# One SBUF buffer shared in turns by the residual sum and the Strassen sums, with the HBM weight sums paced by the SP queue

## The chip, the cores and the metric

The kernel runs on one core of a Trainium2 chip. The metric is device time in microseconds (us): the median of several executions. Besides these there is one profiled execution, from which all traces below come. The engines are named as in the profile: PE (TensorE, matmuls; PEld its weight loads), DVE (VectorE), ACT (ScalarE), POOL (GpSimd), and SP (SyncE, which only issues DMAs here). "SPq", "POOLq" and "ACTq" are the sequencers that issue DMAs. Each engine carries out its own instructions in order.

## The reference

Two layers over x of 512 positions by 1024 features, in float32, each ending in `LayerNorm(ALPHA * h + sublayer(h))` with ALPHA = sqrt(2).

```python
# layer 0: one input projection (6 x 1024 columns) for two branches
q, k, v, g_ret, xb, g_lru = split(h @ w_in)
ret = group_norm(chunked_retention(rope(q), rope(k), v)) * silu(g_ret)   # 8 heads of 128
lru = rg_lru(conv4(xb)) * silu(g_lru)                                    # 8 blocks of 128
h = layer_norm(ALPHA * h + concat(ret, lru) @ w_out)
# layer 1: differential attention, 8 heads, two softmax maps each, value width 256
q, k, v, g = split(h @ w_in)                                             # 4 x 2048 columns
w = softmax(q1 k1) - lam * softmax(q2 k2)                                # causal
o = rms_norm(w @ v) * silu(g)
h = layer_norm(ALPHA * h + o @ w_out)
```

## The kernel before

**Products.** A float32 operand is split into a rounded high part and a low rest (`split`, L142: one ACT cast and one DVE subtraction, L148 and L149), and every product is three matmuls (`mm3`, L151 to L154). Weights lie in HBM as pieces of 128 x 1024 values, 512 KB each, named w0, w1, ... in the order of use. `fetch` (L166) loads a piece on SP into one of two raw buffers (`wraw`) and splits it into one of five pairs (`wsp`). `take(n)` (L181) asks for the next piece and sees to it that n more are on their way. A `t_unit` is one piece: eight k-tiles of three 128x512 matmuls; an `s_unit` is four pieces; an `out_unit` (L222) is one output projection of four pieces (two in layer 0's last parts).

**Order.** PE's and SP's instructions run in the order in which the program text issues them (manual schedule). ACT, DVE and POOL are ordered by the framework's scheduler, which may move an instruction ahead of anything that it doesn't depend on. A planner, `Side` (L48), mixes side jobs into the units: after each k-tile the unit calls `side.tick()`, and at most one waiting job then issues its next piece; a job that yields n is due again n ticks later. `side.need(job)` runs ticks until a job is done. Layer 0 has 512 ticks of its own: 40 t_units of 8, two s_units of 32, and output projections of 32, 32, 16, 16 and 32.

**Layer 0** runs the list `ev` (L254): values, then per head gates, conv inputs, q and k, with retention and RG-LRU as side jobs, and its output projections adding into `y`, a 128 x 4 x 1024 SBUF tile (2 MB, tag "y"). `even_end` (L595) normalizes y, transposes it into `h` (the input of layer 1), multiplies it by ALPHA on ACT (L605) and stores it to `yd` in HBM by eight POOL DMAs (L606).

**Layer 1** runs the list `od` (L270): v and g of heads 0 and 1, q and k of heads 0 to 2, then for g = 1, 2, 3 a "gv" unit, the output projection of a pair of heads, and q and k of the next heads. Attention runs as side jobs. A gv unit (`gates_values`, L733) makes gates and values of two heads by a Strassen-like scheme of seven block products in place of eight. It needs two kinds of sums:

- sums of weight blocks, t1 to t4 (L283 to L286), 24 pieces in all, made in HBM: a copy and then a DMA that accumulates, both issued by POOL from the side job `weight_sums` (L384), which starts at tick 30 and issues one DMA every 10 ticks;
- sums of blocks of h, four of 1 MB (`act_sums`, L695): fourteen DVE and four ACT instructions on 128 x 1024 values, issued all at once after unit g; two half buffers of a tile `st` with tag "y" are used twice each, and four POOL DMAs store the sums to `sd` in HBM. From there `load_sum` (L729) brings two at a time into `sx`, also tag "y": on the ACT queue, at the end of each unit that needs them next and twice within a gv unit.

Since tag "y" is one buffer, y itself stays in HBM during layer 1: each output projection of layer 1 copies its PSUM banks out by ACT (L689) and adds them to `yd` by accumulating POOL DMAs (`add_to_y`, L687, 24 of them). Before the last projection, L849 to L851 load `yd` back into SBUF on SP, and `odd_out` (6, 7) adds the last heads and normalizes (L852).

```python
848    gb1 = ln_params(a["od_ln"], "ln1", *((qkp, n) for n in ("qh", "ql", "kh", "kl")))
849    y = big.tile([P, SB, D], F32, tag="y", name="y2")
850    for sb in range(SB):
851        nc.sync.dma_start(out=y[:, sb], in_=yd[sb])
852    odd_out((6, 7), "oo6", after=odd_end, late=P_LAST)
```

Of the kernel before, what the change touches and what calls it, by code (L numbers as in the profile page):

```python
# [8 lines left out]
F32 = mybir.dt.float32  # L9
# [27 lines left out]
ATT_VALUE = 2  # L37
# [7 lines left out]
SUM_START, SUM_GAP = 30, 10  # L45
# [52 lines left out]
def trunk(ctx: ExitStack, tc: tile.TileContext, a):  # L98
# [123 lines left out]
    def out_unit(mix, y, name, first, before=None, after=None, late=0, keep=None):  # L222
        n = len(mix)
        w = [take(1 if n == 2 else 0) for _ in range(n)]
        for sb in range(SB):
# [10 lines left out]
            for hf, ps in enumerate(pss):  # L236
                if keep is not None:
                    keep(sb, hf, ps)
                    continue
                yy = y[:, sb, hf * HALF:hf * HALF + HALF]  # L240
                with tc.high_priority(late):
                    if first:
                        nc.vector.scalar_tensor_tensor(out=yy, in0=yy, scalar=ALPHA, in1=ps, op0=ALU.mult, op1=ALU.add)
                    else:
                        nc.vector.tensor_tensor(out=yy, in0=ps, in1=yy, op=ALU.add)
                    if late:
                        if hf == 0:
                            st = small.tile([P, 2, 6], F32, tag="bst", name="bst")
                        nc.vector.bn_stats(out=st[:, hf], in_=yy)
                        stats[sb] = st  # L250
# [25 lines left out]
    for kind, i in od:  # L276
        if kind == "o":
            order += [(oo[2 * hd + j], j) for hd in i for j in range(2)]
        elif kind == "gv":
# [4 lines left out]
            for j in range(2):  # L284
                for n, one, two in ((1, b[0, 1], b[0, 0]), (3, b[1, 1], b[0, 1]), (2, b[1, 1], t[1]), (4, b[1, 0], t[2])):
                    sums += [(t[n][j], one[j], None), (t[n][j], two[j], ALU.add)]  # L286
# [97 lines left out]
    def weight_sums():  # L384
        for dst, src, op in sums:
            nc.gpsimd.dma_start(out=dst, in_=src, max_dma_last_dim=4 * D, **({"accum_op": op} if op else {}))  # L386
# [208 lines left out]
    def even_end(sb):  # L595
        pts = list(layer_norm(y, sb, gb0))

        def fin():
            for hf, hv in pts:
# [5 lines left out]
                nc.scalar.activation(out=hv, in_=hv, func=AF.Identity, scale=ALPHA)  # L605
                nc.gpsimd.dma_start(out=yd[sb][:, hf * HALF:hf * HALF + HALF], in_=hv)  # L606
# [72 lines left out]
    def odd_out(hds, name, **kw):  # L679
# [5 lines left out]
        out_unit([t for hd in hds for t in mix_of(om[hd])], y, name, False, before=before, **kw)  # L685

    def add_to_y(sb, hf, ps):  # L687
        t = work(f"oy{sb}{hf}")
        nc.scalar.copy(out=t, in_=ps)  # L689
        nc.gpsimd.dma_start(out=yd[sb][:, hf * HALF:hf * HALF + HALF], in_=t, accum_op=ALU.add)  # L690
# [4 lines left out]
    def act_sums():  # L695
# [3 lines left out]
        def add(t, r, c, op, first=None):  # L699
            for x in range(2):  # L700
                if x or first is None:
                    nc.vector.tensor_tensor(out=t, in0=t, in1=block(r, c, x), op=op)
                else:
                    first(block(r, c, x))

        def less(t, u):
            return lambda b: nc.vector.scalar_tensor_tensor(out=t, in0=u, scalar=-1.0, in1=b, op0=ALU.mult, op1=ALU.subtract)

        def put(k, n):
            split(lows[k], (st[:, k, 0].bitcast(F32R), st[:, k, 1].bitcast(F32R)))  # L710
            nc.gpsimd.dma_start(out=sd[n], in_=st[:, k])

        def difference(t, one, two):
            nc.vector.tensor_tensor(out=t, in0=block(*one, 0), in1=block(*two, 0), op=ALU.subtract)
            nc.vector.tensor_tensor(out=t, in0=t, in1=block(*one, 1), op=ALU.add)
            nc.vector.tensor_tensor(out=t, in0=t, in1=block(*two, 1), op=ALU.subtract)

        st = big.tile([P, 2, 2, KT // 2, 2 * P], F32, tag="y", name="st")
        lows = [st[:, k, 1] for k in range(2)]
        difference(lows[0], (1, 1), (1, 0))  # L720
        add(lows[1], 0, 0, ALU.subtract, less(lows[1], lows[0]))
        put(0, 0)
        add(lows[0], 0, 1, ALU.subtract, less(lows[0], lows[1]))
        put(1, 1)
        put(0, 3)
        difference(lows[1], (0, 0), (1, 0))
        put(1, 2)

    def load_sum(n, k):  # L729
        for j in range(2):  # L730
            nc.scalar.dma_start(out=sx[:, k, :, 2 * j:2 * j + 2].bitcast(F32), in_=sd[n][:, :, 2 * j:2 * j + 2])

    def gates_values(i):  # L733
# [6 lines left out]
        def product(ps, left, start):  # L740
            for j in range(2):
                w = take(2)
# [49 lines left out]
        vt[i] = side.now + ATT_VALUE  # L792
        if i < 3:
            load_sum(1, 0)
            load_sum(2, 1)
# [10 lines left out]

    early = ctx.enter_context(ExitStack())
    extra.update(dict.fromkeys(range(taken[0], taken[0] + EARLY), pool("wx", EARLY, early)))
    for kind, i in od:
        if kind == "v":  # L810
# [10 lines left out]
            if i == 0:  # L821
                early.close()
                qkp = pool("qkp2", 4)
                es = pool("es2", 2)
                mask = load("mask", [P, S], a["mask"], pl=es, bufs=1)
        elif kind == "g":
# [7 lines left out]
            act_sums()  # L834
            sx = big.tile([P, 2, 2, KT // 2, 2 * P], F32R, tag="y", name="sx")
            load_sum(1, 0)
            load_sum(2, 1)
        elif kind == "gv":
            gates_values(i)
        elif kind == "qk":  # L840
            om[i] = mix_pair(f"om{i}") if i < 7 else None
            qk = [[rope(t_unit(h, f"{n}{i}{mp}o"), n, f"{n}{i}{mp}o") for mp in range(2)] for n in "qk"]
# [3 lines left out]
        else:  # L846
            odd_out(i, f"oo{i[0]}", keep=add_to_y)
    gb1 = ln_params(a["od_ln"], "ln1", *((qkp, n) for n in ("qh", "ql", "kh", "kl")))
    y = big.tile([P, SB, D], F32, tag="y", name="y2")  # L849
    for sb in range(SB):  # L850
        nc.sync.dma_start(out=y[:, sb], in_=yd[sb])  # L851
# [84 lines left out]
```

## Time and profile before

| what | value |
|---|---|
| median of 3 runs | 1026.35 us (1025.69 to 1027.76) |
| the profiled execution's own time | 1028.51 us |
| its span in the trace | 1026.7 us |
| mean granted TensorE clock | 0.967 |
| PE busy | 937.8 us (91%), 4255 matmuls |
| DVE, ACT, POOL busy | 724.6, 517.6, 122.4 us |
| HBM read, written | 135.37 MB, 39.85 MB |
| DMA of the SP, POOL, ACT queues | 99.74, 37.75, 12.58 MB |

Busy time of PE is modelled from the matmuls' starts, so a matmul that runs at a lower clock counts as longer busy: at full clock a 128x512 matmul starts 0.23 us after the one before it, and twice that apart where the clock is granted at half. Idle time and clock have to be read together. In a list of waits, "A <- B" says that engine A's instruction stood until B's was done. For a DMA issue, the time to landing runs from its issue to the arrival of its last byte.

### The profile page before, as it was taken

What the parts mean: (1) busy time and instruction counts of PE and PEld (TensorE: products, weight loads), DVE (VectorE), ACT (ScalarE), POOL (GpSimd) and SP (SyncE); (2) the same over time, 40 slices, a digit from 0 to 9 for tenths busy, and PEclk for the clock granted to TensorE, in tenths of its full rate; (3) what the DMA queues carried; (4) which work ended last, traced back from release to release, by engine and by line L of the source; (5) the groups of instructions that cost most, each with busy time, mean ns of one, the idle gap of its engine ahead of it and who ended that gap; (6) DMA issues with size and microseconds to landing.
All of it is one profiled execution on the core that took longest, in us unless ns stands there. A gap on an engine that the chain in (4) does not pass through costs nothing.

```text
span 1026.7 us, 11812 instructions
## 1 busy us (share of the span) xinstructions
PE 937.8 (91%) x4255; PEld 760.9 (74%) x4255; DVE 724.6 (71%) x1197; ACT 517.6 (50%) x829; POOL 122.4 (12%) x202
## 2 busy tenths in 40 slices
PE   7877889999999899899998999899996999999956
PEld 5656767887888788688886887688774887867835
DVE  3654787687867998798688876368754389668447
ACT  3253667656546667434424575443654434755330
POOL 2222200000000000021001220310101201101303
PEclk9889898999999999999999999999998999999978
DMA  9999962141322322324661247662365642454542
GB/s 298 305 308 325 256 178 77 57 138 68 103 93 82 103 93 74 123 93 165 225 226 63 81 142 238 134 163 82 103 220 164 110 143 64 133 193 123 108 139 82
DMA packets 48699, 150.82 MB, mean 147 GB/s; under 512 B 5505, under 2 KB 5633, under 8 KB 48129
## 3 DMA queue, kind: packets, MB, share of 16 engines
q1 hardware_dynamic: 30528, 99.74, 28.8%
q0 software_dynamic: 11584, 37.75, 15.4%
q10 hardware_dynamic: 6528, 12.58, 3.8%
q8 instruction: 33, 0.54, 0.2%
q14 instruction: 26, 0.20, 0.1%
HBM read 135.37 MB, written 39.85 MB: 171 GB/s over the span
## 4 chain that ended last, share of the span: by engine, by line
PE 18%; DVE 14%; DMA 8%; ACT 5%; issue 4%; POOL 2%; ACTq 0%; DVEq 0%; SPq 0%; POOLq 0%
DMA w_r<-in_od_w 2%; DMA w_r<-in_od_wo 2%; PE oo_ps L153 2%; DMA w_r<-t 2%; PE oo_ps L154 2%; PE oo_ps L152 2%; ACT e L637 1%; DMA sd<-st 1%; POOL ars L344 1%; POOL rs_t L343 1%; PE po L152 1%; ACT L637 1%; PE po L154 1%; PE po L153 1%; PE wt L649 1%
## 5 line engine op out<-in xcount | busy, mean ns | idle before, releaser
L668 DVE SCALAR_TENSOR_TENSOR o<-po,ars,og 128x256 f32<-128x256 f32 x32 | 15.5, 484 | 40.2 <-POOL ars L344 39.3
L644 POOL TENSOR_SCALAR zr<-z 128x1 f32<-128x1 f32 x32 | 14.9, 467 | 231.4 <-ACT e L637 231.2
L637 ACT ACTIVATE e<-as,nm 128x128 f32<-128x128 f32 (+3 forms) x64 | 33.3, 525 | 16.5 <-DVE nm L634 16.4
L343 POOL TENSOR_SCALAR rs_t<-bmv 128x1 f32<-128x1 f32 x6 | 3.1, 520 | 319.6 <-DVE bmv L354 312.2
L634 DVE CUSTOM_DVE_ANT_0 as<-as,mask 128x128 f32<-128x128 f32 (+3 forms) x64 | 30.4, 508 | 4.3 <-PE as L154 4.2
L690 POOL DMA_DIRECT2D yd<-oy x24 | 21.6, 903 | 62.4 <-ACT oy L689 49.3
L343 POOL TENSOR_SCALAR rs_t<-ss,zr 128x1 f32<-128x1 f32 x32 | 13.9, 435 | 119.8 <-ACT po L664 110.2
L386 POOL DMA_DIRECT2D t<-in_od_w x36 | 24.4, 725 | 31.1 <-DMA t<-in_od_w 21.1
L689 ACT COPY oy<-oo_ps 128x512 f32<-128x512 f32 x24 | 14.1, 588 | 20.6 <-PE oo_ps L154 18.2
L664 ACT ACTIVATE po<-po 128x256 f32<-128x256 f32 x32 | 12.0, 374 | 21.4 <-PE po L154 20.5
L642 DVE RECIPROCAL zr<-z 128x1 f32<-128x1 f32 x32 | 5.2, 163 | 24.2 <-ACT e L637 23.9
L649 PE MATMUL wt<-ident,e 128*128 128x128 f32 x80 | 14.1, 274 | 7.3 <-DVE e L645 7.3
L344 POOL TENSOR_TENSOR ars<-rs_t,nhalf 128x1 f32<-128x1 f32 x32 | 19.1, 598 | 2.7
L649 PEld LDWEIGHTS wt<-ident,e 128*128 128x128 f32 x80 | 10.1, 140 | 12.4 <-issue 5.1
L386 POOL DMA_DIRECT2D t<-t x12 | 10.0, 830 | 77.2 <-DMA t<-in_od_w 47.4
L645 DVE SCALAR_TENSOR_TENSOR e<-e,zr,e 128x128 f32<-128x128 f32 (+3 forms) x32 | 17.6, 550 | 0.8
L505 DVE SCALAR_TENSOR_TENSOR xc<-xbp,vecs,xc 128x509 f32<-128x509 f32 (+2 forms) x24 | 17.9, 747 | 0.2
L527 DVE SCALAR_TENSOR_TENSOR xc<-t,r 128x512 f32<-128x512 f32 x8 | 5.5, 693 | 16.1 <-ACT r L526 16.1
L462 DVE TENSOR_TENSOR rsd<-rs,dec 128x512 f32<-128x512 f32 (+3 forms) x32 | 15.5, 487 | 1.5 <-PE rs L154 1.4
L673 PEld LDWEIGHTS po<-ident,o 128*128 128x128 f32 x64 | 8.3, 143 | 10.2 <-DVE o L668 7.3
L673 PE MATMUL po<-ident,o 128*128 128x128 f32 x64 | 13.0, 285 | 3.1 <-DVE o L668 2.8
L637 ACT ACT_TABLE_LOAD x9 | 11.5, 1283 | 8.1 <-DVE nm L634 8.0
(2851 smaller groups left out, 3543.5 us busy)
## 6 DMA issues: line engine op xcount, KB each, us to landing
w_r<-in_od_w SPq DMA_DIRECT2D x58, 512.0 KB, 3.4
w_r<-in_ev_w SPq DMA_DIRECT2D x47, 512.0 KB, 4.0
t<-in_od_w POOLq DMA_DIRECT2D x36, 512.0 KB, 10.5
sx<-sd ACTq DMA_DIRECT2D x24, 512.0 KB, 5.2
w_r<-t SPq DMA_DIRECT2D x24, 512.0 KB, 3.4
w_r<-in_ev_wo SPq DMA_DIRECT2D x16, 512.0 KB, 3.3
w_r<-in_od_wo SPq DMA_DIRECT2D x16, 512.0 KB, 3.9
t<-t POOLq DMA_DIRECT2D x12, 512.0 KB, 7.9
```

The lines of the kernel that those rows point to most:

```text
L152: nc.tensor.matmul(out=out, lhsT=l[0], rhs=r[0], start=start, stop=False, **kw)
L153: nc.tensor.matmul(out=out, lhsT=l[0], rhs=r[1], start=False, stop=False, **kw)
L154: nc.tensor.matmul(out=out, lhsT=l[1], rhs=r[0], start=False, stop=stop, **kw)
L343: nc.gpsimd.tensor_scalar(out=t, in0=var, scalar1=scale, scalar2=eps, op0=ALU.mult, op1=ALU.add)
L344: nc.gpsimd.tensor_tensor(out=out, in0=t, in1=nhalf[:, :1], op=ALU.pow)
L386: nc.gpsimd.dma_start(out=dst, in_=src, max_dma_last_dim=4 * D, **({"accum_op": op} if op else {}))
L505: nc.vector.scalar_tensor_tensor(out=xc[:, sh:], in0=xb[:, :S - sh], scalar=conv_w(w, c), in1=xc[:, sh:], op0=ALU.mult, op1=ALU.add)
L634: nc.vector.tensor_tensor_reduce(out=ps[:, :n], in0=ps[:, :n], in1=mask[:, S - n:], scale=-QK_SCALE, scalar=3.0e38, op0=ALU.add, op1=ALU.m ...
L637: nc.scalar.activation(out=e, in_=ps[:, :n], func=AF.Exp, scale=-1.0, bias=nm, accum_out=z[:, mp:mp + 1])
L649: nc.tensor.transpose(out=pt[:, kb * P:kb * P + P], in_=ee[0][:, kb * P:kb * P + P], identity=ident)
L673: nc.tensor.transpose(out=pm[:, i * P:i * P + P], in_=o[:, i * P:i * P + P], identity=ident)
L690: nc.gpsimd.dma_start(out=yd[sb][:, hf * HALF:hf * HALF + HALF], in_=t, accum_op=ALU.add)
```

## The change

1. **Weight sums.** Each of the 24 sums is one step of the side job: its first half is a plain copy from HBM to HBM issued on SP, its second half the accumulating DMA on POOL. The job starts at tick 40 and yields 18 ticks per sum (before: tick 30, and 10 per DMA, 20 per sum).
2. **Sums of h.** `act_sums` becomes a side job that starts after unit v and gives way after every one or two instructions (24 ticks in all, beside the 32 ticks of unit g). Each sum has its own 1 MB buffer in a pool `ss`, which is closed after unit g; then the pools of q and k, which were opened before unit g, are opened in that space. The four stores to `sd` come at the job's end, on SP. The attention mask's load moves behind them.
3. **y.** The ALPHA multiplication and the eight stores at layer 0's end go, and so do the 24 copies and accumulating DMAs of layer 1. y and `sx` take turns in the buffer by plain SP transfers: `store_y` (4 x 512 KB to `yd`) after the first q/k unit that follows unit g or an output projection, `swap_in` (allocate `sx`, load two sums on SP) after the third; `current` loads y back (4 x 512 KB) ahead of the projections (0, 1), (2, 3) and (4, 5), after their weights are taken. DVE adds each PSUM bank to y, the first projection with the factor ALPHA. After (4, 5) y stays in SBUF, and (6, 7) adds to it without a load.
4. **Smaller.** Products of a gv unit take three pieces ahead and not two, and attention may use its values four ticks after it and not two.

```diff
-ATT_VALUE = 2
+ATT_VALUE, GV_VALUE = 2, 4
-SUM_START, SUM_GAP = 30, 10
+SUM_START, SUM_GAP = 40, 18
...
-    def out_unit(mix, y, name, first, before=None, after=None, late=0, keep=None):
+    def out_unit(mix, y, name, first, before=None, after=None, late=0):
         n = len(mix)
         w = [take(1 if n == 2 else 0) for _ in range(n)]
+        y = y() if callable(y) else y
...
     def weight_sums():
-        for dst, src, op in sums:
-            nc.gpsimd.dma_start(out=dst, in_=src, max_dma_last_dim=4 * D, **({"accum_op": op} if op else {}))
+        for dst, one, two in sums:
+            nc.sync.dma_start(out=dst, in_=one)
+            nc.gpsimd.dma_start(out=dst, in_=two, max_dma_last_dim=4 * D, accum_op=ALU.add)
             yield SUM_GAP
...
-                nc.scalar.activation(out=hv, in_=hv, func=AF.Identity, scale=ALPHA)
-                nc.gpsimd.dma_start(out=yd[sb][:, hf * HALF:hf * HALF + HALF], in_=hv)
                 yield 1
...
-        out_unit([t for hd in hds for t in mix_of(om[hd])], y, name, False, before=before, **kw)
-    def add_to_y(sb, hf, ps):
-        t = work(f"oy{sb}{hf}")
-        nc.scalar.copy(out=t, in_=ps)
-        nc.gpsimd.dma_start(out=yd[sb][:, hf * HALF:hf * HALF + HALF], in_=t, accum_op=ALU.add)
+        def current():
+            nonlocal y
+            if 6 not in hds:
+                y = big.tile([P, SB, D], F32, tag="y", name="y")
+                for sb in range(SB):
+                    nc.sync.dma_start(out=y[:, sb], in_=yd[sb])
+            return y
+
+        out_unit([t for hd in hds for t in mix_of(om[hd])], current, name, 0 in hds, before=before, **kw)
+
+    def store_y():
+        for sb in range(SB):
+            nc.sync.dma_start(out=yd[sb], in_=y[:, sb])
...
+        st = [ss.tile([P, 2, KT // 2, 2 * P], F32, tag=f"ss{n}", name=f"ss{n}") for n in range(4)]
+        low = [t[:, 1] for t in st]
+        yield from difference(low[0], (1, 1), (1, 0))
+        yield from less(low[1], low[0], block(0, 0, 0), block(0, 0, 1))
+        yield from put(0)
+        yield from less(low[3], low[1], block(0, 1, 0), block(0, 1, 1))
+        yield from put(1)
+        yield from put(3)
+        yield from difference(low[2], (0, 0), (1, 0))
+        yield from put(2)
+        for n, t in enumerate(st):
+            nc.sync.dma_start(out=sd[n], in_=t)
...
-                w = take(2)
+                w = take(3)
...
-        vt[i] = side.now + ATT_VALUE
-        if i < 3:
-            load_sum(1, 0)
-            load_sum(2, 1)
+        vt[i] = side.now + GV_VALUE
...
+    def swap_in():
+        nonlocal sx
+        sx = big.tile([P, 2, 2, KT // 2, 2 * P], F32R, tag="y", name="sx")
+        load_sum(1, 0, nc.sync)
+        load_sum(2, 1, nc.sync)
+
+    def qk_unit(n, name):
+        r = rope(t_unit(h, name), n, name)
+        if later:
+            later.pop(0)()
+        return r
...
-                qkp = pool("qkp2", 4)
-                es = pool("es2", 2)
-                mask = load("mask", [P, S], a["mask"], pl=es, bufs=1)
+                scratch = ctx.enter_context(ExitStack())
+                ss = pool("ss", 1, scratch)
+                summed = side.add(act_sums(), "sums", 1)
...
             s_unit(h, f"og{i}", False, evac)
-            act_sums()
-            sx = big.tile([P, 2, 2, KT // 2, 2 * P], F32R, tag="y", name="sx")
-            load_sum(1, 0)
-            load_sum(2, 1)
+            side.need(summed)
+            scratch.close()
+            qkp = pool("qkp2", 4)
+            es = pool("es2", 2)
+            mask = load("mask", [P, S], a["mask"], pl=es, bufs=1)
+            later[:] = [store_y, no_op, swap_in]
...
-            odd_out(i, f"oo{i[0]}", keep=add_to_y)
+            odd_out(i, f"oo{i[0]}")
+            if i[0] < 4:
+                later[:] = [store_y, no_op, swap_in]
     gb1 = ln_params(a["od_ln"], "ln1", *((qkp, n) for n in ("qh", "ql", "kh", "kl")))
-    y = big.tile([P, SB, D], F32, tag="y", name="y2")
-    for sb in range(SB):
-        nc.sync.dma_start(out=y[:, sb], in_=yd[sb])
     odd_out((6, 7), "oo6", after=odd_end, late=P_LAST)
```

47 lines of the change are left out of this document (19 added, 28 removed).

## The prediction

> **What bounds the kernel now**
>
> I read the stages first, then who made PE wait, then the DMA behind each wait. The stage table gives, for each stretch of the span, the busy time of the engines (with instructions), the granted TensorE clock, the mean busy share of the DMA engines and what they moved.
>
> ```profile
> core 0: us, PE busy (x) PEld busy (x) DVE busy (x) ACT busy (x) POOL busy (x), PEclk, DMA share, GB/s
> 0.00:43.00 43.00, 33.57 (x103) 23.92 (x104) 17.82 (x45) 11.97 (x18) 10.32 (x20) 0.88 0.98 307
> 43.00:180.00 137.00, 115.85 (x482) 93.18 (x481) 94.17 (x138) 80.98 (x105) 22.84 (x33) 0.91 0.80 232
> 180.00:459.00 279.00, 271.12 (x1235) 223.80 (x1233) 224.31 (x336) 163.00 (x217) 3.98 (x6) 1.00 0.28 93
> 459.00:588.00 129.00, 125.19 (x589) 103.13 (x587) 105.67 (x170) 54.41 (x99) 17.33 (x30) 0.99 0.44 152
> 640.00:673.00 33.00, 29.60 (x146) 23.77 (x145) 13.28 (x23) 15.48 (x31) 9.38 (x16) 1.00 0.62 137
> 766.00:817.00 51.00, 41.34 (x174) 30.95 (x173) 20.03 (x29) 23.44 (x40) 9.69 (x16) 0.90 0.57 147
> 949.00:977.00 28.00, 27.96 (x139) 23.16 (x138) 13.23 (x37) 10.73 (x30) 9.43 (x15) 1.00 0.59 115
> 977.00:999.00 22.00, 9.69 (x33) 6.74 (x34) 8.61 (x14) 6.40 (x10) 1.58 (x4) 0.69 0.49 141
> ```
>
> The third row, 180 to 459 us, is layer 0 in its steady state: PE is 97% busy at full clock with DMA at 0.28, and 279 us for 1235 matmuls are 0.226 us each. DVE is at 224 of 279 us there, 80%, so PE sets the pace. The first 180 us look different: DMA at 0.98 and then 0.80, a clock of 0.88 and 0.91, and 482 matmuls in 137 us, 0.284 us each. So DMA bounds the first stage, not PE. The last row, 977 to 999 us, has PE busy for 9.7 of 22 us at clock 0.69; the two output units at 640 and 766 us lie in between.
>
> What PE waited for (total us, times, longest):
>
> ```profile
> PE oo_ps L152 <- ACT w158h L145: 10.5, 1, 10.5
> PE rs L152 <- DVE rsd L462: 9.8, 3, 8.8
> PE wt L649 <- DVE e L645: 7.3, 4, 3.3
> PE pr L152 <- ACT xc0h L148: 5.9, 1, 5.9
> PE oo_ps L152 <- ACT w126h L145: 3.9, 1, 3.9
> PE ev_ps L152 <- ACT w3h L148: 3.1, 1, 3.1
> ```
>
> Five of these six lead back to a late weight. The first, w158h, and w126h and w3h are casts of weights that had not landed. The retention product `rs` and the conv product `pr` need ACT and DVE results that stood in those engines' order behind a weight split: ACT itself waited longest, in the first 180 us, for w14,
>
> ```profile
> ACT w14h L148 <- DMA w_r<-in_ev_w: 10.3, 1, 10.3
> ```
>
> and the 8.8 us of `rs` fall in that wait. Who fills the DMA engines at that time is seen in POOL's own issues (duration in ns, first and last start in us):
>
> ```profile
> L386 POOL DMA_DIRECT2D t<-in_od_w x36: 515/808/878, 1.3 to 128.9; - x36
> ```
>
> All 36 transfers that read weights for the sums of layer 1 start between 1.3 and 128.9 us, though the planner asked for them over 480 ticks: nothing ties them to PE. Landing times (issue to last byte) on the two sides:
>
> ```profile
> w_r<-in_od_w SPq DMA_DIRECT2D x58, 512.0 KB, 3.4
> w_r<-in_ev_w SPq DMA_DIRECT2D x47, 512.0 KB, 4.0
> t<-in_od_w POOLq DMA_DIRECT2D x36, 512.0 KB, 10.5
> ...
> sd<-st POOLq DMA_DIRECT2D x4, 1024.0 KB, 5.7
> ```
>
> **The change, part by part**
>
> The profiled execution took 1028.51 us with a span of 1026.7; the median is 1026.35. I take differences from the trace and subtract them from the median. Two runs of this kernel can differ by 0.2%, 2 us, so less is no change.
>
> *Weight sums.* The first copy is issued at tick 40, after the value unit (32 ticks) and one t_unit (8), and the last at tick 40 + 23 x 18 = 454 of 512. The copy now sits in SP's order, and SP is held to PE by its two raw buffers; POOL's accumulating half waits for its copy. So the bunch of the first 130 us is drawn out over nearly all of layer 0. On POOL, nothing but later sums is queued behind that wait until layer 0's normalization, which starts after tick 480. On SP, the copies need no buffer and wait for nothing.
>
> First gain: the value unit. When PE starts, and how it starts after a pause, is in the timeline of PE (start, duration in us; in brackets the idle time before and its cause):
>
> ```profile
> 5.00 0.79 PE L152 MATMUL ev_ps<-w0h,xh 128*128 128x512 f32 x1 [0.57 <-ACT w0h L148]
> ...
> 504.89 0.39 PE L154 MATMUL og_ps<-w71h,hl 128*128 128x512 f32 x1
> ...
> 976.57 0.39 PE L154 MATMUL as<-k71oh,q71ol 128*128 128x512 f32 x1
> 987.42 0.79 PE L152 MATMUL oo_ps<-w158h,om6h 128*128 128x512 f32 x1 [10.46 <-ACT w158h L145]
> 988.74 0.79 PE L153 MATMUL oo_ps<-w158l,om6h 128*128 128x512 f32 x1 [0.53 <-DVE w158l L146]
> ...
> 992.36 0.40 PE L152 MATMUL po<-ov30h,w72h 128*128 128x256 f32 x1
> ```
>
> 96 matmuls from 5.0 us on at 0.226 are 21.7 us. A cold start costs about 2.4 us: after the 10.46 us pause, the nine 512-column matmuls from 987.42 to 992.36 took 4.94 us in place of 2.04, of which 0.53 was another wait. That puts the unit's end at 29.1 us; before, it fills the first row of the table (96 of the 103 matmuls, the other seven being the warm-up), 43 us, so 13.9 go; SP needs x and four weights by then, 4 MB, which at the 307 GB/s of the first row take 13 us once POOL is silent. I take **-13** (bounds -14, and -9 where the loads of x and w keep a third of the loss). The Trainium skill ("TensorE: Matmul & The Clock Gate", Part 1) says that after about 3.4 us without work the array runs at half clock until it has been busy for 3.4 us; that makes, as an estimate, 1.7 us per pause, and the sum would be 0.7 us better in this term and 0.7 us worse in the end term, and the trace's slow stretch of over 4 us is the longer of the two.
>
> Second gain: 43 to 180 us. At the steady 0.226, 482 matmuls take 109 us, 28 less. But sums still run beside them, at a lower density. I take **-20** (bounds -28, and -10 where two thirds of the loss stay with the sums that run here).
>
> A cost: 180 to 459 us ran with no sums and now gets most of them. The two queues' total work:
>
> ```profile
> q1 hardware_dynamic: 30528, 99.74, 28.8%
> q0 software_dynamic: 11584, 37.75, 15.4%
> ```
>
> 99.74 MB in 28.8% of 1026.7 us is 2.96 us per MB on SP's queue, and 37.75 MB in 15.4% is 4.19 on POOL's. 24 copies and 24 accumulations of 0.52 MB are 12.6 MB each, 37 + 53 = 90 us. Spread over the some 370 us from tick 40 to 454, the DMA share rises by 0.24, from 0.28 to about 0.52. The stage from 459 to 588 ran at 0.44 and kept PE at 97%. So the price is small: **+5**, between 0 and +15; the upper end is 24 times 0.6 us. What hides it is the prefetch of two pieces, 2 x 24 x 0.226 = 10.9 us, against 3.4 us of landing.
>
> *Sums of h.* Before, the sums stood in DVE's and ACT's order for their own stores:
>
> ```profile
>   ACT q00oh L148: 5.6, 1
>   DVE st L707: 3.8, 1
>   DVE st L714: 2.9, 1
> ```
>
> Those 3.8 and 2.9 us of DVE go, since each sum has its own buffer, and fourteen instructions are spread over unit g. They delayed the first ropes, and the longest wait of `wt`, 3.3 us, comes from the DVE backlog after them. What is late next: the pools of q and k lie where the sums lie, so the first cast of q (ACT) waits for the four stores, and SP carries these stores, 4 MB, and the mask ahead of the third q/k weight. SP can't issue the last stores before DVE has made the last sum, near the end of unit g, whose last matmul in the timeline above starts at 504.89 us; one MB took 5.7 us to land, so two in a row end near 515, and the weight behind them some 3 us later, when PE wants it (505 + 10.9). Behind it come the 2 MB of y. So a stall of 0 to 8 us on one side and the old stall with its backlog, 8 us, on the other: **0**, between -8 and +8.
>
> *y by plain transfers.* DVE's adds replace ACT's copies:
>
> ```profile
> L245 DVE TENSOR_TENSOR y<-eo_ps,y x8: 677/686/692, 440.2 to 464.1; 128x512 f32<-128x512 f32 x8
> L689 ACT COPY oy<-oo_ps x24: 582/588/591, 647.7 to 975.6; 128x512 f32<-128x512 f32 x24
> ```
>
> 24 adds of 0.69 are 16.5 us more DVE work, 24 x 0.59 = 14.1 us less on ACT. In the output units DVE is busy 13.3 of 33, 20 of 51 and 13.2 of 28 us, so the adds are hidden; if they weren't, they would cost 5.5 us per unit. 24 POOL issues go as well. The units themselves: (4, 5), which started with its weights loaded and no `sx` load beside it, ran 139 matmuls in 28 us, 0.201 each. At that rate the stretches at 640 and 766 us would take 29.4 and 35 us, 3.6 and 16 less. In the changed kernel the `sx` loads are no longer issued at the start of these units, and a third piece is taken ahead. In their place SP loads 2 MB of y, behind the unit's weights but held until the last matmul that reads `sx`; queued behind it on SP are the weights of the next heads, and DVE's first add waits for it. PE spends over 5 us on the first pair of banks, and a block of y is half an `sd` store (5.7 us). `store_y` and `swap_in` then stand between weights, 2 MB each, where two pieces of prefetch cover 10.9 us. I take **-13** (bounds -20 and -4).
>
> *The end.* SP's issues before the last unit:
>
> ```profile
> 960.10 21.44 SPq L851 DMA_DIRECT2D y<-yd  x4
> 981.64 8.72 SPq L174 DMA_DIRECT2D w_r<-in_od_wo  x4
> ```
>
> The load of y was held from 960 to 981.6 us by the last accumulation into `yd`, and the last four weights were queued behind it: hence the 10.46 us. Now there is no load, and the weights can be fetched while (4, 5) runs, as far as the five buffers go. Gone: 10.46 us, 2.9 us of slow clock and 0.5 us of w158l; attention of head 7 then comes closer. **-13** (bounds -14 and -9).
>
> Sum: -13 - 20 + 5 + 0 - 13 - 13 = -54, or 972 us. All good ends together give -84, 942; all bad ends -9, 1017.
>
> **The rivals**
>
> *The cost belongs to the sums, not to their bunching.* The first two stages lose 13.9 + 28 = 42 us to 24 sums, 1.75 us each. If a sum costs PE as much wherever it runs, because an in-order ACT or DVE stands behind any late weight, the 42 us only move into the steady stage. What stays is 0 - 13 - 13: 1000 us. For it speaks DVE at 80% in the steady stage, with little room to catch up; against it the stretch at DMA 0.44 without such loss. The Trainium skill ("DMA: Bandwidth & Descriptors", Issuing engines are not separate DMA queues) says that all queues feed the same sixteen DMA engines and that another issuing engine saves only issue time; by that rule alone the move of the copies to SP brings nothing, and only the later start can.
>
> *More than that.* Layer 0 reaches its steady rate at once and the accumulations cost nothing: -28 in place of -20, 0 in place of +5, and some of the stall at the sums: 955 us or less.
>
> *Weights stand behind copies (slower).* A copy on SP goes ahead of the next weight in the same queue. The cover is 10.9 us less 3.4 of landing, 7.5 us; beyond that PE waits. The same copies took 10.5 us to land on POOL's queue. If they do so on SP, each exposes 3 us, 24 x 3 = 72 us: 972 + 72 = 1044 us. It decides once a copy keeps its weight back by more than 7.5 us, and the kernel is slower than before from about 9.8. Against it: those 10.5 us were measured with several transfers in flight at a share near 1.
>
> *It does nothing.* SP might run ahead and bunch the copies as before, or the waits at the ends be replaced by equal ones: 1020 to 1028. The two raw buffers speak against it.
>
> **How the numbers follow**
>
> The forecast, 957 to 987 with 972 the likeliest, gets 0.55; "cost belongs to the sums", near 1000, 0.20; "more than that", below 957, 0.12; slower, 1044, 0.07; nothing, 0.06, half of it faster by over 2 us. The range of 8 in 10 runs from 946 to 1003: it leaves out the lowest part of the third case, the slower ones and the upper part of the second. Faster 0.55 + 0.20 + 0.12 + 0.03 = 0.90, the same 0.03, slower 0.07.
>
> **What would show it**
>
> The value unit ends near 30 us, POOL's first sum is issued after about 35 us and the last near 400; DMA stays below 0.7 from 45 us to 450 with PE over 95% busy, and `pr <- xc0h` and `rs <- rsd` fall below 2 us. The output units take 28 to 32 us, `w158h` leaves the list, and the last load of y is gone. I am wrong in the first part if ACT still waits over 5 us for weights of layer 0, or if PE's busy share from 180 to 459 us falls below 93%; in the second, if the third weight of q and k after unit g, or one behind `store_y` and `swap_in`, heads the list of PE's waits, or if the adds in the output units wait for y.

## The result and the profile after

The changed kernel takes 978.35 us (median of 4 runs, 977.99 to 979.96); the kernel before, on the same chip, 1026.02 us. The ratio is 0.9546 (95% interval 0.9511 to 0.9581), a gain of some 48 us. The profiled execution took 977.99 us with a span of 976.2 and a mean granted clock of 0.984. The forecast of 972 us was 6 us too low, and the time lies inside the range of 957 to 987 us.

The stage table of the kernel after, cut where its own units end, so that the rows hold the same work as those shown of before (value unit; up to w20; the rest of layer 0; units v and g of layer 1 and q and k of heads 0 to 2; the output units of heads (0, 1), (2, 3), (4, 5) and (6, 7)):

```profile
core 0: us, PE busy (x) PEld busy (x) DVE busy (x) ACT busy (x) POOL busy (x), PEclk, DMA share, GB/s
0.00:29.70 29.70, 27.97 (x103) 21.54 (x104) 17.38 (x45) 12.38 (x19) 0.29 (x5) 1.00 0.69 227
29.70:138.80 109.10, 107.03 (x483) 88.00 (x482) 93.94 (x139) 80.57 (x105) 7.62 (x9) 1.00 0.70 206
138.80:430.00 291.20, 277.40 (x1232) 227.39 (x1231) 224.29 (x336) 164.11 (x216) 14.37 (x19) 0.98 0.48 143
430.00:558.00 128.00, 125.29 (x591) 103.47 (x590) 104.60 (x170) 51.30 (x92) 10.62 (x20) 0.99 0.44 154
608.70:641.30 32.60, 29.44 (x146) 23.62 (x145) 17.74 (x30) 11.99 (x25) 3.51 (x9) 1.00 0.47 177
737.50:781.00 43.50, 38.78 (x171) 30.50 (x170) 21.93 (x33) 16.28 (x29) 3.51 (x9) 0.92 0.45 162
913.40:940.30 26.90, 26.90 (x136) 22.65 (x135) 18.62 (x42) 9.72 (x25) 2.78 (x7) 1.00 0.26 88
940.30:967.00 26.70, 26.68 (x131) 22.05 (x130) 23.73 (x44) 5.25 (x13) 6.87 (x11) 1.00 0.15 57
```

Read it against the rows of before. The first 103 matmuls take 29.7 us in place of 43 and the next 483 take 109.1 in place of 137 (482 there), both at full clock: DMA has left 0.98 and 0.80 for 0.70. The third row gives some of this back: 1232 matmuls take 291.2 us where 1235 took 279, with DMA up from 0.28 to 0.48. The unit of (2, 3), 737 to 781 us, still has a clock of 0.92; in the last row PE never stops.

Sums per stage can hide which moment gained, so I also read the start of the last matmul of each unit in PE's timeline of both kernels. The kernel after, for the value unit, q and k after unit g (w83), (4, 5) and (6, 7):

```profile
29.58 0.39 PE L154 MATMUL ev_ps<-w3h,xl 128*128 128x512 f32 x1
...
557.66 0.39 PE L154 MATMUL k21o_ps<-hh,w83l 128*128 128x512 f32 x1
...
939.89 0.40 PE L154 MATMUL oo_ps<-w157h,om5l 128*128 128x512 f32 x1
...
966.59 0.39 PE L154 MATMUL oo_ps<-w161h,om7l 128*128 128x512 f32 x1
```

The same four of the kernel before:

```profile
42.99 0.39 PE L154 MATMUL ev_ps<-w3h,xl 128*128 128x512 f32 x1
...
587.77 0.39 PE L154 MATMUL k21o_ps<-hh,w83l 128*128 128x512 f32 x1
...
975.20 0.39 PE L154 MATMUL oo_ps<-w157h,om5l 128*128 128x512 f32 x1
...
1017.50 0.39 PE L154 MATMUL oo_ps<-w161h,om7l 128*128 128x512 f32 x1
```

The difference at a piece is the lead that the kernel after has by then; the difference of two leads is what it won or lost between them. With more rows of the same two timelines:

| until the last matmul of | before, us | after, us | lead, us |
|---|---|---|---|
| value unit (w3) | 42.99 | 29.58 | 13.4 |
| w18 (k of layer 0) | 166.28 | 124.81 | 41.5 |
| w67 (a value piece of layer 1) | 482.47 | 453.80 | 28.7 |
| w83 (q and k after unit g) | 587.77 | 557.66 | 30.1 |
| w101, unit (0, 1) | 672.6 | 641.12 | 31.5 |
| gv2b, w121 | 766.24 | 737.35 | 28.9 |
| w127, unit (2, 3) | 816.22 | 780.65 | 35.6 |
| w157, unit (4, 5) | 975.20 | 939.89 | 35.3 |
| w161, unit (6, 7) | 1017.50 | 966.59 | 50.9 |

The issues of the weight sums, SP's copies and POOL's accumulations, and the landing of the copies:

```profile
L384 SPq DMA_DIRECT2D t<-in_od_w x24: 494/495/1434, 25.9 to 344.2; - x24
...
L385 POOL DMA_DIRECT2D t<-in_od_w x12: 812/814/1161, 32.1 to 312.0; - x12
L385 POOL DMA_DIRECT2D t<-t x12: 812/823/837, 52.9 to 349.2; - x12
```

```profile
t<-in_od_w SPq DMA_DIRECT2D x24, 512.0 KB, 6.0
```

They are spread over 323 us, where the 36 reading transfers of before took 128. What PE waited for now:

```profile
PE ro L152 <- ACT r31h L148: 4.3, 1, 4.3
PE wt L646 <- DVE e L642: 3.9, 3, 2.2
...
PE rs L152 <- ACT k2h L148: 1.5, 1, 1.5
PE gv2b L152 <- ACT w121h L148: 1.5, 1, 1.5
PE oo_ps L152 <- ACT w101h L145: 1.4, 1, 1.4
PE oo_ps L153 <- DVE w127l L146: 1.2, 1, 1.2
```

`w158h` (10.5 us), `rs <- rsd` with its 8.8 and `pr <- xc0h` with its 5.9 are gone from the top. The longest wait of all is now 4.3 us, at 202 us.

### The profile page after: what moved, and what is told of

It reads as the page before. It is cut to its first block, busy times and chain, and to the rows that moved or that the text cites. A ratio compares the mean times of both kernels' runs of the same rounds, so it can differ in the third digit from the quotient of the medians.

```text
span 976.2 us, 11727 instructions
## 1 busy us (share of the span) xinstructions
PE 926.3 (95%) x4255; PEld 757.8 (78%) x4255; DVE 736.4 (75%) x1221; ACT 501.9 (51%) x798; POOL 81.7 (8%) x142
## 3 DMA queue, kind: packets, MB, share of 16 engines
q1 hardware_dynamic: 38016, 133.29, 38.9%
q0 software_dynamic: 3456, 12.58, 7.4%
## 4 chain that ended last, share of the span: by engine, by line
PE 56%; DVE 17%; ACT 11%; DMA 9%; issue 4%; POOL 1%; SPq 0%; DVEq 0%; ACTq 0%; POOLq 0%
DMA w_r<-in_ev_w 4%; DMA w_r<-in_od_w 2%; PE oo_ps L153 2%; PE oo_ps L154 2%; PE oo_ps L152 2%; PE ev_ps L152 2%; PE ev_ps L153 2%; PE ev_ps L154 2%; DMA w_r<-t 2%; ACT e L634 2%; DMA w_r<-in_ev_wo 1%; PE xb_ps L152 1%; PE xb_ps L153 1%; PE xb_ps L154 1%; ACT L634 1%
## 5 line engine op out<-in xcount | busy, mean ns | idle before, releaser
L243 DVE TENSOR_TENSOR y<-oo_ps,y 128x512 f32<-128x512 f32 x24 | 16.3, 686 | 6.0 <-PE oo_ps L154 6.0
L385 POOL DMA_DIRECT2D t<-in_od_w x12 | 10.4, 863 | 121.7 <-DMA t<-in_od_w 121.7
L634 ACT ACTIVATION_READ_ACCUMULATOR e<-as,nm 128x1 f32 x64 | 12.5, 196 | 0.0
L520 DVE TENSOR_TENSOR xbp<-xbp,xc 128x512 f32<-128x512 f32 x8 | 5.5, 690 | 9.0 <-ACT xbp L517 9.0
```

Source lines behind the costliest of these rows:

```text
L385: nc.gpsimd.dma_start(out=dst, in_=two, max_dma_last_dim=4 * D, accum_op=ALU.add)
L634: nc.scalar.activation(out=e, in_=ps[:, :n], func=AF.Exp, scale=-1.0, bias=nm, accum_out=z[:, mp:mp + 1])
```

## Experiments

My theory: the sums cost PE less when they are issued in PE's order, because it is DMA crowding that makes a weight late, and an in-order ACT or DVE behind that weight passes the delay on; and the end gains what the last load of y had cost. The first rival: the cost belongs to each sum and merely moves. All edits are to the kernel after. They were measured in three groups, each beside runs of before of its own, to which the ratios refer: no_sums, pool_sums, pool_paced and reload_end (before: 1025.07 us), no_sums_ticks, late_sums, sums_at_once and take2 (1027.47), and sp_dense, late_free, small_undone and after_again (1028.21). after_again is the kernel after once more: 976.38 us, ratio 0.9497 (0.947 to 0.9525), beside the first 978.35 and 0.9546. So two groups can differ by 0.5%, 5 us, in the ratio of one kernel.

**no_sums.** All 24 sums left out, so that layer 1 reads one block in place of the sum of two (it leaves out work that the result needs, and only its time is read).

```diff
-                    sums.append((t[n][j], one[j], two[j]))
+                    t[n][j] = one[j]
```

> The changed kernel without any weight sums: the gv units read unsummed weight blocks in their place (this leaves out the 24 sums; times only). Theory A, the 12.7 us of lead that the changed kernel loses between 172 and 460 us are lost to the sums that now run there: 978.4 - 12 = 966 us, lead kept at 40 or more. Rival B, the loss is a shifted order of ACT and DVE work that has nothing to do with the sums: 976 to 979 us.

Measured: 955.73 us, ratio 0.9311 (0.9274 to 0.9348), 22.6 us below the kernel after and 10 beyond theory A. By the end of layer 0 it leads the kernel after by 21.5 us. But 4.2 of these arise at one piece, w58, some 50 us after the last sum had been issued: leaving the job out also changes the order in which the planner deals out its ticks. A run below, no_sums_ticks, takes that apart.

**pool_sums.** The sums of before put back, the rest as after.

```diff
-SUM_START, SUM_GAP = 40, 18
+SUM_START, SUM_GAP = 30, 10
...
-            nc.sync.dma_start(out=dst, in_=one)
+            nc.gpsimd.dma_start(out=dst, in_=one, max_dma_last_dim=4 * D)
+            yield SUM_GAP
```

> The changed kernel with the weight sums as before: both halves on POOL, tick 30, one DMA per 10 ticks, free to run ahead. Theory A, the sums' part of the change is worth the lead at the end of layer 0, 28.7 us: 1007 us, with DMA near 1 in the first 130 us and PE late in the value unit. Rival B, what counts in layer 0 is also POOL's removed stores or another part: clearly below 1000 us.

Measured: 1003.34 us, ratio 0.9779 (0.9739 to 0.9818): 25.0 us slower than after, close to theory A. So this part of the change is worth 25 us, about half of the gain. In the traces pool_sums is 26.9 us behind after at the end of layer 0, where before is 28.9 behind. The copies run ahead of PE once more:

```profile
L384 POOL DMA_DIRECT2D t<-in_od_w x24: 515/654/857, 1.3 to 127.0; - x24
```

**pool_paced.** First half of each sum on POOL as before, but tied to PE's order by a 4 KB transfer on SP into the same tile.

```diff
-            nc.sync.dma_start(out=dst, in_=one)
+            nc.sync.dma_start(out=dst[:16, :64], in_=one[:16, :64])
+            nc.gpsimd.dma_start(out=dst, in_=one, max_dma_last_dim=4 * D)
```

> The changed kernel with the sums' first half back on POOL's queue, but held to the same ticks by a 4 KB transfer on SP into the same tile that it has to wait for. Theory A, only when a sum starts matters, not which queue carries it: 976 to 981 us. Rival C, the queue matters (weights stand behind copies on SP, or share packets with POOL's): 4 us or more away from 978, either side.

Measured: 976.16 us, ratio 0.9515 (0.9484 to 0.9546); the kernel after has 0.9546 (0.9511 to 0.9581), and the two intervals overlap. The issue times are those of after, from the other queue:

```profile
L385 POOL DMA_DIRECT2D t<-in_od_w x24: 522/542/845, 30.6 to 353.1; - x24
```

So it is when a copy is issued that counts; who issues it makes no difference that shows. The Trainium skill ("DMA: Bandwidth & Descriptors", Issuing engines are not separate DMA queues) says that another issuing engine saves issue time alone; this pair agrees with it, 976.16 beside 978.35 us. It also answers a doubt of the prediction: a copy ahead of a weight in SP's own queue costs nothing that shows.

**reload_end.** y stored after (4, 5) and loaded back ahead of (6, 7).

```diff
+    store_y()
+    y = big.tile([P, SB, D], F32, tag="y", name="y")
+    for sb in range(SB):
+        nc.sync.dma_start(out=y[:, sb], in_=yd[sb])
     odd_out((6, 7), "oo6", after=odd_end, late=P_LAST)
```

> The changed kernel, but after the projection (4, 5) y is stored to HBM and loaded back ahead of (6, 7), as plain SP transfers. Theory A, the last 15.6 us of lead come from the missing load of y with four weights queued behind it on SP: at least as much comes back, store and load one after the other, 978 + 16 to 22 = 994 to 1000 us, with w158h at the head of PE's waits. Rival B, the gain at the end comes from ACT and POOL being free of the copies and accumulations: under 985 us.

Measured: 996.54 us, ratio 0.9711 (0.9674 to 0.9748), 18.2 us slower than after; in its profile 18.9 us are lost to the kernel after in the last unit. SP's queue and PE's longest wait in reload_end:

```profile
921.77 21.08 SPq L694 DMA_DIRECT2D yd<-y  x4
945.27 1.75 SPq L876 DMA_DIRECT2D y<-yd  x4
947.05 12.18 SPq L174 DMA_DIRECT2D w_r<-in_od_wo  x4
```

```profile
PE oo_ps L152 <- ACT w158h L145: 13.5, 1, 13.5
```

And SP's queue in the kernel after:

```profile
903.89 1.85 SPq L687 DMA_DIRECT2D y<-yd  x4
...
908.68 30.50 SPq L174 DMA_DIRECT2D w_r<-in_od_wo  x4
```

The store of a finished y holds SP until the unit before has added its last bank (921.77 plus 21.08 us), and the last four weights stand behind it. Without it they are issued from 908.68 us on, one as each buffer comes free, while PE still runs (4, 5). The run holds a store that before did not have, so its 18.2 us are not exactly the price of the old load (15.6 us between the traces of before and after).

**no_sums_ticks.** No sums, as in the first run, but the job keeps its place in the plan.

```diff
-        for dst, one, two in sums:
-            nc.sync.dma_start(out=dst, in_=one)
-            nc.gpsimd.dma_start(out=dst, in_=two, max_dma_last_dim=4 * D, accum_op=ALU.add)
+        for _ in range(24):
             yield SUM_GAP
```

> The run without weight sums again (gv units read unsummed blocks, the 24 sums are left out), but the side job still takes its 24 ticks, with nothing in them. Theory A, the 22.6 us that the run without sums was ahead are all DMA: 955 to 958 us. Rival D, part of them is the planner's order, since a tick that a sum takes moves every side job on PE behind it: later than 958 us, by as much as the order is worth; 978 if all of it.

Measured: 960.38 us, ratio 0.9347 (0.9311 to 0.9382). With the same plan the transfers alone cost 978.35 - 960.38 = 18.0 us, 0.75 us per sum (by the ratios 20, and 15 against after_again). The 4.7 us to no_sums fit the step seen at w58, but the two intervals overlap, so that the order has a price of its own is likely and not shown. This gives the prediction's price a measured counterpart: bunched from the start, the sums cost 1003.34 - 960.38 = 43.0 us, 1.8 us each; spread, 0.75.

**sp_dense.** The sums of after with a gap of 5 ticks in place of 18: SP's copies, but in a bunch behind the value unit.

```diff
-SUM_START, SUM_GAP = 40, 18
+SUM_START, SUM_GAP = 40, 5
```

> The changed kernel with its sums bunched: still copied by SP in PE's order, but one per 5 ticks from tick 40 on, 120 ticks or some 85 us in all. Theory A, bunching is what costs: DMA near 1 in that stretch, 24 sums cost 1.5 us or more each and not 0.8, 990 to 1005 us. Rival B, it is only the tie to PE's order that matters, a copy that SP issues in its place among the weights does no harm: 976 to 982 us.

Measured: 985.42 us, ratio 0.9588 (0.9561 to 0.9616), 9 us above after_again: between the two theories, and outside both of their bands. It costs 25.0 us over no_sums_ticks (1.04 us per sum). Three kernels in the same two stretches, 30 to 172 us and 172 to 430 us, columns as in the stage table; first the kernel after, then no_sums_ticks, then sp_dense:

```profile
30.00:172.00 142.00, 139.94 (x634) 115.56 (x633) 117.84 (x175) 101.12 (x133) 8.44 (x10) 1.00 0.60 178
172.00:430.00 258.00, 244.20 (x1079) 199.58 (x1078) 200.39 (x299) 143.26 (x188) 13.56 (x18) 0.97 0.51 151
```

```profile
30.00:172.00 142.00, 139.93 (x635) 115.90 (x635) 116.91 (x175) 100.21 (x131) 0.00 (x0) 1.00 0.31 106
172.00:430.00 258.00, 252.93 (x1150) 209.08 (x1149) 214.97 (x322) 149.43 (x197) 3.53 (x8) 0.99 0.29 98
```

```profile
30.00:172.00 142.00, 121.90 (x505) 96.95 (x504) 97.16 (x143) 81.72 (x108) 20.23 (x24) 0.92 0.94 270
172.00:430.00 258.00, 255.76 (x1160) 211.86 (x1159) 210.91 (x315) 157.41 (x207) 1.30 (x2) 1.00 0.29 98
```

And pool_sums, where the first 30 us belong to it as well:

```profile
0.00:30.00 30.00, 24.27 (x71) 17.51 (x72) 9.69 (x18) 9.88 (x16) 8.02 (x17) 0.89 0.96 314
30.00:172.00 142.00, 117.41 (x496) 94.59 (x495) 95.72 (x156) 78.95 (x102) 25.09 (x37) 0.92 0.86 247
```

Read the matmuls. At DMA 0.60 PE gets through 634 in the first stretch, as many as with no sums at all (635); at 0.94 it gets through 505. In the second stretch the order is turned round: after, with its sums still running, 1079, sp_dense, done with them, 1160. So the spread sums cost nothing in the first stretch and 71 matmuls in the second. pool_sums has 71 matmuls in its first 30 us where sp_dense has 103: it starts its copies at 1.3 us and not at 26, and has lost 11.0 us to the kernel after by the end of the value unit. So of the 25 us of pool_sums some 11 come from the sums' early start, beside the value unit; sp_dense, whose sums start behind it, is 7 us slower than after (9 by after_again). What the rest is made of was not taken apart.

**late_sums** and **late_free.** The sums spread further, into layer 1: in late_sums a gap of 34 ticks, the accumulation 12 ticks behind its copy, and a group of its own in the planner; in late_free a gap of 30, the same 12, and no tick taken from other jobs (the planner runs the sums and goes on).

```diff
-SUM_START, SUM_GAP = 40, 18
+SUM_START, SUM_GAP = 40, 34
...
             nc.sync.dma_start(out=dst, in_=one)
+            yield 12
             nc.gpsimd.dma_start(out=dst, in_=two, max_dma_last_dim=4 * D, accum_op=ALU.add)
-            yield SUM_GAP
+            yield SUM_GAP - 12
```

> The changed kernel with the sums at half the density: one per 34 ticks in a group of its own, so that they run on through layer 1, the accumulating half issued 12 ticks after the copy. Theory A, a sum costs PE less where DMA is less dense: 970 us or less, DMA share from 172 to 430 us near 0.42. Rival E, a sum costs about 0.9 us wherever it runs, and in layer 1 POOL's waits for copies hold attention's small instructions: 978 us or more.

> The changed kernel with one sum per 30 ticks, running on into layer 1, the accumulating half 12 ticks after the copy, and the sums' job taking no tick from the other side jobs. Theory A, both the density of DMA and the tick cost time, up to 18 and 4.7 us by the two runs without sums: 962 to 972 us. Rival E, a sum costs the same wherever it runs: 975 to 980 us.

Measured: late_sums 973.39 us, ratio 0.9477 (0.9428 to 0.9527); late_free 973.47 us, ratio 0.9469 (0.9435 to 0.9503). Both lie between the bands of their theories, and both intervals overlap that of after_again, so neither is shown to be faster. The traces tell where the thinner stretch went. late_free leads after by 6.6 us at the end of layer 0 and by nothing (-0.2) at the last matmul of w98. From the last matmul of w83 to that of w101 both kernels take 88.4 us, where after takes 83.5, after_again 85.5 and no_sums_ticks, with no sums at all, 85.4. late_free's last sums run in the first half of this stretch, up to 598 us, beside the loads of `sx` and the stores and loads of y. But most of its loss comes in the output unit (0, 1) behind them, at a clock of 0.91 against 1.00 in after, so how the sums cause it stays open.

**sums_at_once, take2, small_undone.** The sums of h issued at once behind unit g, as before, though with four buffers; the lookahead of the gv units back from 3 pieces to 2; both.

```diff
-                summed = side.add(act_sums(), "sums", 1)
...
-            side.need(summed)
+            list(act_sums())
```

```diff
-                w = take(3)
+                w = take(2)
```

> The changed kernel with the sums of h issued at once after unit g, as before, still in four buffers and stored on SP. Theory A, the spreading itself is worth little, since the lead rises by only 1 us around unit g: 977 to 983 us. Rival F, spreading keeps DVE from a backlog of 17 us and the third q/k weight from standing behind 4 MB of late stores: 986 us or more, with a stall of PE after unit g.

> The changed kernel with two and not three pieces taken ahead in the gv units. Theory A, the gain of 5 us around the second output unit is the third piece ahead: 981 to 985 us, PE waits for w126 again. Rival G, it is the missing load of sx at the start of that unit: 977 to 980 us.

> The changed kernel with two small parts undone at once: two pieces ahead in the gv units, and the sums of h issued at once after unit g. Theory A, neither part is worth anything that can be measured: within 3 us of the changed kernel. Rival F, either part holds a gain: 5 us or more slower. Rival H, undoing them is a gain, as the single runs of 974 and 976 us hint: 3 us or more faster.

> The changed kernel once more, as the measure for the other three on the same chip: 975 to 981 us by all theories.

Measured: sums_at_once 975.73 us, ratio 0.9513 (0.9461 to 0.9564); take2 973.64, ratio 0.948 (0.9428 to 0.9531); small_undone, both undone, 972.37, ratio 0.9457 (0.9417 to 0.9497). All three intervals overlap that of after_again (0.947 to 0.9525). So rival F and theory A of take2 fail, and neither of these two parts of the change is worth anything that can be measured here. small_undone's median is 4.0 us below after_again, as rival H has it, but its six runs lie between 967.26 and 979.82 us: none of the variants is shown to beat the kernel after either.

## Why the prediction was right, and where its terms were off

The sum, -54, became -48.0 by the medians (1026.35, from which the forecast was taken, to 978.35), -50.5 by the profiled executions (1028.51 to 977.99). Term by term, from the leads:

| step of the prediction | forecast (bounds) | the two traces |
|---|---|---|
| value unit | -13 (-14, -9) | -13.4 |
| 43 to 180 us (to w18) | -20 (-28, -10) | -28.1 |
| 180 to 459 us gets the sums (to w67) | +5 (0, +15) | +12.8 |
| sums of h (to w83) | 0 (-8, +8) | -1.4 |
| output units (to w157) | -13 (-20, -4) | -5.2 |
| the end (to w161) | -13 (-14, -9) | -15.6 |

The lead is the same at w18 and at w20, where the second stage ends. So the direction held in every step where one was forecast, but three sizes were off by some 8 us each (-8, +8, +8) and the last by 2.6 (-2.6). That they largely cancel is luck. Behind two of them the working was wrong too: the cover in the price of the sums, and the rate taken for the output units.

*Weight sums.* The working gave -20 for the second stage since "sums still run beside them". They did, and cost nothing there: 634 matmuls with them, 635 without. The price that I had put half into each stage fell due in the later one, +12.8 in place of +5. The two together are -15.3 where I had -15. The step that failed is the cover, two pieces of prefetch against 3.4 us of landing: it is counted for PE, and ACT and DVE have no such cover. Against no_sums_ticks, the kernel after loses its time in layer 0 in two moments. It is 0.5 us behind when w29 begins (187.57 us), 8.7 when w31 does (208 us), 8.9 at w48, 13.4 at w49 (326 us), and 14.7 at the end of layer 0. The first moment, from 176 to 206 us:

```profile
176.00:206.00 30.00, 23.56 (x101) 18.68 (x100) 19.52 (x28) 10.22 (x16) 3.31 (x4) 0.91 0.90 259
```

POOL, ACT and PE in that stretch, a fence each:

```profile
188.91 0.83 POOL L385 DMA_DIRECT2D t<-t  x1 [9.87 <-DMA t<-t]
189.43 1.16 POOL L385 DMA_DIRECT2D t<-in_od_w  x1
192.78 0.81 POOL L385 DMA_DIRECT2D t<-in_od_w  x1 [2.18 <-DMA t<-in_od_w]
```

```profile
200.92 1.04 ACT L148 CAST w34h<-w_r 128x1024 fp32r<-128x1024 f32 x1 [5.30 <-DMA w_r<-in_ev_w]
201.87 0.51 ACT L148 CAST r31h<-rsd 128x384 fp32r<-128x384 f32 x1
```

```profile
202.43 0.69 PE L152 MATMUL ro<-r31h,ev01h 128*128 128x384 f32 x1 [4.27 <-ACT r31h L148]
```

Three accumulations that had been held came within 4 us, the DMA share rose to 0.90, the weight w34 was late, ACT stood at its cast for 5.3 us, and behind it in ACT's order stood `r31h`, for which PE waited 4.27 us. PE itself wants w34 only at 230.35 us. This is the chain of before in small; an average of 0.48 holds moments of 0.90. In the second moment, 313 to 327 us, PE waits 2.5 us for a DVE result (`rsd`), with the clock at 0.88. The trace of after_again has both waits again (3.5 and 2.5 us). But before and pool_sums have the second too, at the same `pi` product (2.5 and 2.4 us), when their sums are long done, so it can't be put down to the transfers alone. Nor does a high share cost by itself, as an earlier stretch of the kernel after shows:

```profile
50.00:70.00 20.00, 20.00 (x90) 16.57 (x89) 16.68 (x23) 14.25 (x17) 1.65 (x2) 1.00 1.05 344
```

Here PE waited for nothing. My own sign of being wrong, an ACT wait of over 5 us for a weight of layer 0, was met (7.4 us for w5, 5.3 for w34, 5.1 for w32); PE lost nothing by the first of them. PE's share in the stage stayed at 277.4 of 291.2 us, 95%. Three other signs failed: the last sum is issued at 349 us and not near 400, DMA does not stay below 0.7 (the row above), and the unit of (2, 3) takes 43.5 us and not 28 to 32.

*The rival "the cost belongs to the sums".* It was priced at 42 us, 1.75 us per sum, that only move. Measured, the bunch costs 43.0 us, so the price was right; spread, 18.0 us remain, so 25 do not move. The rival was some two fifths right. My own terms had left some 14 (42 less 33, plus 5).

*Sums of h.* Little (-1.4; -3.5 in the trace of after_again), close to the 0 of the forecast, but that 0 was a balance of two prices and neither was there. The stall that I feared does not show in PE's list. The old one, which I had put at 8 us, was not there to be won: in before, PE's waits from 459 to 588 us come to 3.7 us in all, in after to 2.6 in the same units.

*Output units.* Here the argument itself failed: I took the rate of (4, 5), which had its weights loaded, for the stretches of the other two, where weights still come late. (0, 1) took 32.6 us and gained next to nothing; (2, 3) took 43.5, and by the leads gained 6.7; between them, up to w121, 2.6 were lost. In (0, 1) PE is busy 29.44 us, just the 29.4 that I had, and the rest is idle: 2.2 us for the fourth weight, 1.0 for `om2l`. In (2, 3) PE waits 1.9 us each for w125 and w127, and the clock is 0.92. SP's queue and PE around (0, 1), which begins at 608.8 us:

```profile
609.21 0.33 SPq L174 DMA_DIRECT2D w_r<-in_od_wo  x1
609.64 1.79 SPq L687 DMA_DIRECT2D y<-yd  x4
```

```profile
614.10 0.50 PE L152 MATMUL oo_ps<-w101h,om1h 128*128 128x512 f32 x1 [1.38 <-ACT w101h L145]
615.42 0.50 PE L153 MATMUL oo_ps<-w101l,om1h 128*128 128x512 f32 x1 [0.82 <-DVE w101l L146]
```

The last weight of the unit is issued only once the unit has begun, 3.5 us before PE wants it (at 612.7) and 4.9 before PE gets it. SP had been held by buffers: in its own list of waits from 590 to 612 us, 5.8 us go to the split of w97, 3.8 to that of w96 and 2.5 to that of w99. So a third piece of lookahead should not bring it sooner, and take2, with two, is no slower. That the number of buffers is the cause is read from these waits; a run with more buffers was not tried. The fear on the other side, a late y, did not come: no wait of PE leads to it. The trace of after_again gives the same 5.2 us for this step. The y transfers by themselves were not undone apart from the end, so their share of the 5.2 us stays open.

*The end.* -15.6, against a lower bound of -14. The row of before shows the difference:

```profile
977.00:1018.00 41.00, 28.58 (x125) 22.29 (x125) 25.55 (x45) 8.79 (x16) 6.64 (x12) 0.83 0.33 102
```

PE was idle for 41.0 - 28.6 = 12.4 us, of which I had 11.0 (10.46 and 0.53), and its 125 matmuls took 0.229 us each against 0.204 after (26.68 for 131), 3.1 us, where I had 2.9. (Those 2.9 hold the 0.53 that stand beside them in the forecast; the slow clock alone is 2.4 by the same lines.) reload_end brings the cost back, and the wait for w158h with it.

The two large parts undone one at a time give 25.0 + 18.2 = 43.2 us, against a gain of 48. What stays open: what makes the second moment, whether an order of ACT's work that keeps the activations ahead of a late weight would win back part of what the spread sums still cost (no run changed it), and whether any spreading of these sums beats the one that was made.

## What to carry to other kernels

A background transfer that no wait ties to the busy engine runs as early as it can, and here it filled the DMA engines when the main stream needed them most. Tied to the order of the busy engine, by whichever queue, and spread over the stage, the same bytes cost less than half as much (some 18 us in place of 43; tied and still dense, 25). Prefetch that covers the busy engine does not cover an engine that works in order behind the same weight: look at what stands behind a late weight there. Estimate such a price by what remains with the work left out *and its place in the plan kept*, since taking a job out also moves what is planned around it (4.7 us here, just within the noise). When a queue's prefetch ends at a transfer that needs a finished result, look first at what is queued behind that transfer: that was 16 to 18 us at the end, while a third piece of lookahead, which by SP's waits the buffers could not follow, gave nothing that shows.

## What the hardware showed that was not expected

Per MB, an accumulating DMA takes about twice as much of the engines' time as a plain one here. The kernel after has only accumulations on POOL's queue, so the two can be told apart (packets, MB, share of 16 engines over 976.2 us); the third line is POOL's queue in pool_paced, over 974.7 us, with 24 plain copies beside the same accumulations:

```profile
q1 hardware_dynamic: 38016, 133.29, 38.9%
q0 software_dynamic: 3456, 12.58, 7.4%
...
q0 software_dynamic: 6912, 25.17, 11.3%
```

38.9% of 976.2 us over 133.29 MB is 2.85 us per MB; 7.4% over 12.58 MB is 5.74. It is not the queue or the way from HBM to HBM: in pool_paced 11.3% of 974.7 us are 110 us. If the accumulations take the same 72 there, 38 are left for 12.58 MB of plain copies, as an estimate 3.0 us per MB on the same queue. The prediction had taken 4.19 from the mixture on POOL's queue before. These 12.58 MB are 9% of the two queues' bytes and 16% of their time. From 176 to 206 us POOL's queue moved 2.10 MB and took 37.8% of the engines' time, SP's 5.67 MB and 51.8%. What of the price belongs to the reading of the old value and what to the crowd around these transfers isn't separated here.
